# Moving a norm's scale and shift behind a gather, hinting one branch, and reordering the last norm

## The chip, the cores and the metric

The kernel runs on one core of a Trainium2 chip. Times are device microseconds (us) of one launch. The engines are TensorE (PE; its weight loads are PEld), VectorE (DVE), ScalarE (ACT), GpSimd (POOL) and SyncE (SP), which here only issues DMAs. A program with branches runs on every engine's own sequencer; PEq, DVEq and so on name these queues.

## The reference, cut to what matters

One decoder layer on 512 tokens of width 1024, in float32. A token mixer (gated MLP and dilated attention) gives `mix`; then:

```
x = layer_norm(ALPHA * x + g1 * mix, ln1_g, ln1_b)
h = layer_norm(x) * (1 + sc2) + sh2          # second norm, modulated per column
logits = h @ w_router + b_router             # 32 experts, the 4 best of each token
y = sum over the 4 experts of weight * expert(h)      # clamped SwiGLU, 3 matrices of 1024 x 1024
x = layer_norm(ALPHA * x + g2 * y, ln2_g, ln2_b)      # the last norm
```

Only a token's four experts need its row; the kernel reads all 96 weight matrices (4 MB each) once.

## The kernel before, in words

**Routing stage (540 to 635 us).** `layer` works on four blocks of 128 tokens, r = 0 to 3. `mix(r)` is the last projection on TensorE; `norms(r)` makes the first norm, stores ALPHA * x to the DRAM sum `ysum`, and leaves the plain second norm in `h`; `route(r)` transposes `h` on TensorE for the router matmul (whose weights already hold the column scale `sc2`, and whose bias holds `sh2`), then finds the four experts and the slot of every token in its expert's list, on VectorE. For the experts, GpSimd multiplies and shifts `h` in place by rows `sc2` and `sh2` that were broadcast to 128 partitions (L822, L823, names `h<-h,row_sc` and `h<-h,row_sh`), and SP stores it to the DRAM tensor `h2d` (L824). After block 3 the slot table is turned into `gidx` (L946), row numbers for indirect DMAs. The order on each engine in this stage is a scheduler's, by the order of the code and its priorities.

**Experts (635 to 1859 us).** The order of PE, ACT, DVE and SP is as written. For each expert GpSimd gathers up to 128 rows of `h2d` into `xrow` (L1044); `tr_x` transposes them in eight pieces on TensorE (L1057) into two PSUM tiles `ptm` and copies each with one ScalarE copy into `xT` (L1062). `gate`, `up` and `down` multiply with weights that SP's DMAs bring into a ring of 17 buffers of 1 MB (L1024); a buffer is refilled when its last matmul has read it. An expert with up to 64 rows takes `narrow`, one with more takes `wide`; a wide one with over 128 rows takes further blocks (`further`), which gather, transpose and multiply again. The choice is an `If` on a register, labelled `expert{e}`; every engine branches (L1356). `hint(label, ...)` places an instruction on TensorE that names a coming branch; the branches of experts 1 to 31 and of further blocks have one, that of expert 0 has none. While an expert multiplies, `next_rows` already transposes the next one's rows.

**The last norm.** For expert 31 the object `fin` (class `Finish`) loads four blocks of `ysum` rows, x[0] to x[3], by then complete but for expert 31, and normalizes them while expert 31 multiplies. `spread` takes mean and variance on VectorE (`BN_STATS`, L1275) and the root on ScalarE (L1277); `scale` does both steps of the norm on VectorE (L1283, L1284), `scale_act` one pass on ScalarE (L1290) and two on GpSimd (L1291, L1292); `store` writes the rows out. `early` (after the gate) does this for r = 0, 1 with ScalarE and GpSimd, `middle` (in `next_rows`, ahead of `down`) for r = 2, 3 on VectorE. In `y_out`, `add` then joins expert 31's result with the gathered rows that it belongs to, normalizes them and scatters them over `out` (L1333).

Of the kernel before, what the change touches and what calls it, by code (L numbers as in the profile page):

```python
# [9 lines left out]
F32 = mybir.dt.float32  # L10
# [4 lines left out]
AF = mybir.ActivationFunctionType  # L15
ALU = mybir.AluOpType
AX = mybir.AxisListType.X
ET = mybir.EngineType
# [3 lines left out]
P = 128  # L22
H = P // 2
T = 512
D = 1024
KT = D // P
# [43 lines left out]
def layer(tc, I, out, dump=None, n_exp=NE):  # L70
    nc = tc.nc
    V, S, G, PE, SP = nc.vector, nc.scalar, nc.gpsimd, nc.tensor, nc.sync
# [14 lines left out]
    ident = cst[:, :P]  # L87
# [10 lines left out]
    gidx = cp.tile([P, P], I32, name="gidx")  # L98
    wslot = cp.tile([P, P], F32, name="wslot")
# [600 lines left out]
    def row(nm, src):  # L700
        rows[nm] = r4("row_" + nm, 1)
        SP.dma_start(rows[nm], src[0].partition_broadcast(P))

    col2 = f.tile([P, 2, KT], F32, name="col2")
    for i in range(2):
        SP.dma_start(col2[:, i], rowd[1 + i].rearrange("(k p) -> p k", p=P))
    wr = f.tile([P, KT, NE], F32, name="wr")
# [10 lines left out]
    row("sc2", rowd[1:2])  # L718
    row("sh2", rowd[2:3])
# [93 lines left out]
    def route(r):  # L813
# [8 lines left out]
        G.tensor_tensor(h, h, rows["sc2"], op=ALU.mult)  # L822
        G.tensor_tensor(h, h, rows["sh2"], op=ALU.add)  # L823
# [27 lines left out]
        PE.matmul(pcnt, oneb, ohb_, start=r == 0, stop=r == 3)  # L851
# [129 lines left out]
def moe(tc, nc, I, E, main, env):  # L981
    (xrow, land, splA, landB, h2d, ysum, gidx, wslot, gidx2, wslot2, balld, selb, levw, ident, ysv, g2, g2s, yrow, y_init,
     out, epsT, after, last_dve, last_act) = (env[n] for n in (
         "xrow land splA landB h2d ysum gidx wslot gidx2 wslot2 balld selb levw ident ysv g2 g2s yrow y_init out epsT "
# [74 lines left out]
    def tr_x(src, dst):  # L1059
        for a in range(2):  # L1060
            transposes(src[:, 512 * a:512 * a + 512], 4, ptm[a])
            S.copy(dst[:, 4 * a:4 * a + 4], ptm[a])  # L1062
# [139 lines left out]
    def wide(e, lev, levP):  # L1202
        rows_ahead(e, levP)
        gate(e, xT, pg, ga, False, label=f"further{e}_0")
        further(e, 0, lev)
        for q in range(4):
            free(12 * e + q)
        if fin:
            fin.early()
        up(e, xT, pu, ga, aT, False, label=f"further{e}_1")  # L1210
        further(e, 1, lev)
        for q in range(4, 8):
            free(12 * e + q)
        next_rows(e)
        down(e, aT, po, ga, False, free=free, label=f"expert{e + 1}" if e + 1 < E else None)
        y_out(e, 0, po, yrow, False)

    def narrow(e):
        gate(e, xT, pg, ga, True, free)
        if fin:  # L1220
            fin.early()
        up(e, xT, pu, ga, aT, True, free, label=f"expert{e + 1}" if e + 1 < E else None)
        next_rows(e)
        down(e, aT, po, ga, True, free=free)
        y_out(e, 0, po, yrow, True)

    def next_rows(e):
        if e + 1 < E:
            tr_x(xrow, xT)
            if e + 2 < E:  # L1230
                gather(xrow, e + 2, 0)
        if fin:
            fin.middle()
# [7 lines left out]
    class Finish:  # L1241


        def __init__(self):
# [19 lines left out]
            self.mv = [sb.tile([P, 2], F32, name=f"fmv{i}") for i in range(5)]  # L1264
            self.rs, self.nb = (sb.tile([P, 5], F32, name=n) for n in ("frs", "fnb"))
# [27 lines left out]

        def early(self):
            for r in range(2):
                self.spread(r, self.x[r])
            for r in range(2):
                self.scale_act(r, self.x[r])
                self.store(r)

        def middle(self):
            self.fetch(0)
            for r in (2, 3):
                self.spread(r, self.x[r])
                self.scale(r, self.x[r])
                self.store(r)
# [89 lines left out]
```

## Time and profile before

| what | us |
|---|---|
| median of 3 runs | 1881.35 (1880.34 to 1883.35) |
| the profiled execution's own time | 1875.77 |
| its span, first to last instruction | 1874.0 |
| TensorE busy | 1746.6 (93% of the span) |
| VectorE, ScalarE, GpSimd busy | 547.0, 382.3, 201.7 |
| mean granted TensorE clock | 0.974 of full speed |

A busy TensorE says little here, since matmuls are pipelined and weight loads may hold them up; what matters is in which stretches TensorE stands still, and what it then waits for. The DMA rate by slices shows which stretches of the expert loop are fed at the DMA's full rate (some 400 GB/s) and which are not.

### The profile page before, as it was taken

The page shows a single profiled execution, that of the slowest core. Times are in us where ns is not written, and L with a number is a line of the kernel's source. Part 1 is how long each engine was busy: PE and PEld are TensorE (multiplying, and loading weights), DVE is VectorE, ACT ScalarE, POOL GpSimd, SP SyncE. Part 2 cuts the span into 40 slices and gives each one's busy share as a digit, 9 for nine tenths or more (in the row PEclk, how much of TensorE's full clock was granted, in tenths as well). Part 3 has the DMA queues.
Part 4 walks back from the last instruction along what each step waited for, and adds up shares of the span by engine and source line. Part 5 has one row for each costly group of instructions (what it writes and reads, how often), then busy time and mean ns, then how long its engine had stood idle before and what let it go on. Part 6 is the DMA issues. An engine that isn't in the chain of part 4 may idle for free. (4 is left out here: it accounts for less than half of the span.)

```text
span 1874.0 us, 20331 instructions
## 1 busy us (share of the span) xinstructions
PE 1746.6 (93%) x7590; PEld 991.6 (53%) x7590; DVE 547.0 (29%) x901; ACT 382.3 (20%) x745; POOL 201.7 (11%) x152
## 2 busy tenths in 40 slices
PE   6999999999997699999999999998899999899985
PEld 5777778788775444434444444443344444344432
DVE  7546656463279411111111111111011110111115
ACT  3533426255544200100000000011010000000001
POOL 2100000005023300110010001010100000001002
PEclk9999999999999699999999999999999999999998
DMA  8526352423253996999999999999971599949993
GB/s 281 197 88 210 109 191 75 174 68 105 85 187 136 352 366 238 404 404 404 398 390 399 346 380 375 364 399 404 402 284 32 198 401 395 351 170 326 406 384 120
DMA packets 159146, 515.40 MB, mean 275 GB/s; under 512 B 18298, under 2 KB 22858, under 8 KB 158870
## 3 DMA queue, kind: packets, MB, share of 16 engines
q1 hardware_dynamic: 147030, 490.74, 68.3%
q0 software_dynamic: 11840, 21.34, 4.6%
q8 instruction: 128, 2.10, 0.5%
q14 instruction: 148, 1.21, 0.2%
HBM read 504.21 MB, written 23.02 MB: 281 GB/s over the span
## 5 line engine op out<-in xcount | busy, mean ns | idle before, releaser
L1097 ACT ACTIVATE ga<-ga 128x512 f32<-128x512 f32 (+1 forms) x36 | 28.7, 796 | 573.8 <-DVE ga L1096 396.4
L1149 PE MATMUL po<-land,aT 128*128 128x512 f32 x320 | 141.5, 595 | 1.1 <-DVEq L1191 1.1
L166 PE MATMUL mm<-b,splA 128*128 128x512 f32 x352 | 138.8, 394 | 0.0
L167 PE MATMUL mm<-b,splA 128*128 128x512 f32 x352 | 137.9, 392 | 0.0
L168 PE MATMUL mm<-b,splA 128*128 128x512 f32 x352 | 137.8, 392 | 0.0
L1123 PE MATMUL pu<-land,xT 128*64 128x256 f32 x1024 | 129.2, 395 | 8.4 <-DMA land<-in_w_up_dram 8.4
L1091 PE MATMUL pg<-land,xT 128*128 128x512 f32 x288 | 127.7, 599 | 5.1 <-issue 5.1
L1126 PE MATMUL pu<-land,xT 128*128 128x512 f32 x288 | 128.8, 592 | 0.0
L111 DVE TENSOR_TENSOR splA<-land,splA 128x1024 fp32r<-128x1024 f32 x70 | 88.0, 1259 | 130.4 <-ACT splA L110 130.0
L1096 DVE TENSOR_SCALAR ga<-pg 128x512 f32<-128x512 f32 x44 | 30.4, 692 | 317.2 <-PE pg L1091 159.3
L1100 DVE TENSOR_SCALAR pu<-pu 128x256 f32<-128x256 f32 (+1 forms) x64 | 34.1, 533 | 297.6 <-PE pu L1126 160.9
L1088 PE MATMUL pg<-land,xT 128*64 128x512 f32 x504 | 115.3, 608 | 2.6 <-DMA land<-in_w_gate_dram 2.6
L1146 PE MATMUL po<-land,aT 128*64 128x512 f32 x448 | 105.1, 607 | 7.6 <-ACT aT L1107 7.6
L110 ACT CAST splA<-land 128x1024 fp32r<-128x1024 f32 x72 | 75.4, 1051 | 178.1 <-PE mm L168 142.7
L1123 PEld LDWEIGHTS pu<-land,xT 128*64 128x64 f32 x1024 | 74.4, 142 | 53.1 <-DMA land<-in_w_up_dram 13.6
L1107 ACT COPY aT<-ptm 128x256 f32<-128x256 f32 (+1 forms) x64 | 28.9, 451 | 357.8 <-PE ptm L1057 357.8
L1149 PEld LDWEIGHTS po<-land,aT 128*128 128x128 f32 x320 | 59.4, 190 | 70.3 <-issue 67.9
L1091 PEld LDWEIGHTS pg<-land,xT 128*128 128x128 f32 x288 | 55.2, 192 | 72.9 <-issue 70.4
L1044 POOL DMA_INDIRECT xrow<-h2d,gidx x32 | 34.0, 1061 | 541.7 <-PE ptm L1057 530.2
L1126 PEld LDWEIGHTS pu<-land,xT 128*128 128x128 f32 x288 | 53.6, 190 | 66.0 <-issue 64.6
L166 PEld LDWEIGHTS mm<-b,splA 128*128 128x128 f32 x352 | 66.2, 188 | 17.0 <-ACT splA L110 2.6
L1088 PEld LDWEIGHTS pg<-land,xT 128*64 128x64 f32 x504 | 37.0, 140 | 71.2 <-issue 62.4
(379 smaller groups left out, 2514.1 us busy)
## 6 DMA issues: line engine op xcount, KB each, us to landing
land<-in_w_up_dram SPq DMA_DIRECT2D x100, 1024.0 KB, 15.2
land<-in_w_gate_dram SPq DMA_DIRECT2D x99, 1024.0 KB, 18.1
land<-in_w_down_dram SPq DMA_DIRECT2D x96, 1024.0 KB, 18.6
splA<-in_w_down_dram SPq DMA_DIRECT2D x32, 1024.0 KB, 16.4
land<-in_w_in_dram SPq DMA_DIRECT2D x30, 1024.0 KB, 5.2
splA<-in_w_gate_dram SPq DMA_DIRECT2D x29, 1024.0 KB, 20.1
splA<-in_w_up_dram SPq DMA_DIRECT2D x28, 1024.0 KB, 15.8
land<-in_w_ada_dram SPq DMA_DIRECT2D x24, 1024.0 KB, 6.2
```

The costliest lines, as they stand in the source:

```text
L110: hi = S.copy(w[:, 0], src)
L111: return hi, eng.tensor_tensor(w[:, 1], src, w[:, 0].bitcast(F32), op=ALU.subtract)
L166: PE.matmul(o, l[0], r[0], start=start, stop=False)
L167: PE.matmul(o, l[0], r[1], start=False, stop=False)
L168: return PE.matmul(o, l[1], r[0], start=False, stop=stop)
L1088: PE.matmul(r[h], x[:, kt, :H], w[:, :, h], start=False, stop=kt == KT - 1)
L1091: PE.matmul(o[st], x[:, kt], w[:, 512 * st:512 * st + 512], start=False, stop=kt == KT - 1)
L1100: V.tensor_scalar(o, o, LIMIT, -LIMIT, op0=ALU.min, op1=ALU.max)
L1123: PE.matmul(o[st][H * h:H * h + H, :256], x[:, kt, :H], w[:, 256 * h:256 * h + 256], start=False, stop=kt == KT - 1)
L1126: PE.matmul(o[st], x[:, kt], w, start=False, stop=kt == KT - 1)
L1146: end = PE.matmul(o[0][H * n:H * n + H], a[:, 2 * st + b, H * h:H * h + H], wn, start=ft == 0, stop=ft == KT - 1)
L1149: end = PE.matmul(o[n], a[:, ft], wn, start=ft == 0, stop=ft == KT - 1)
```

## The change

Three edits. (1) GpSimd's two passes over `h` and the two row broadcasts go; `h2d` gets the plain second norm, and `tr_x` applies scale and shift while it copies transposed rows: since columns lie on partitions there, the factors are per-partition values, kept in `colh`, a copy of `col2` in a pool that lives on. The first PSUM tile is copied by four ScalarE passes of 128x128, the second by four VectorE passes. (2) A hint for `expert0` stands behind the last count matmul of block 3. (3) In `Finish`, `early` finishes block 0 only; `middle`, now between the next rows and `down`, scales block 1 on VectorE and takes block 2's mean and variance by two ScalarE passes with sums (`spread_act`); `late`, behind `down`, does block 3's on ScalarE and scales 2 and 3 on VectorE.

```diff
+    colh = cp.tile([P, 2, KT], F32, name="colh")
...
+    V.tensor_copy(colh, col2)
...
-    row("sc2", rowd[1:2])
-    row("sh2", rowd[2:3])
...
-        G.tensor_tensor(h, h, rows["sc2"], op=ALU.mult)
-        G.tensor_tensor(h, h, rows["sh2"], op=ALU.add)
         SP.dma_start(h2v[:, r], h)
...
+        cnt = PE.matmul(pcnt, oneb, ohb_, start=r == 0, stop=r == 3)
+        if r == 3:
+            with after(cnt):
+                tc.mark_branch_hint_location("expert0", engines=[ET.PE])
...
     def tr_x(src, dst):
         for a in range(2):
             transposes(src[:, 512 * a:512 * a + 512], 4, ptm[a])
-            S.copy(dst[:, 4 * a:4 * a + 4], ptm[a])
+            for i in range(4):
+                kt = 4 * a + i
+                if a:
+                    V.tensor_scalar(dst[:, kt], ptm[a][:, i], colh[:, 0, kt:kt + 1], colh[:, 1, kt:kt + 1],
+                                    op0=ALU.mult, op1=ALU.add)
+                else:
+                    S.activation(dst[:, kt], ptm[a][:, i], AF.Identity, scale=colh[:, 0, kt:kt + 1],
+                                 bias=colh[:, 1, kt:kt + 1])
...
     def narrow(e):
         gate(e, xT, pg, ga, True, free)
         if fin:
             fin.early()
         up(e, xT, pu, ga, aT, True, free, label=f"expert{e + 1}" if e + 1 < E else None)
         next_rows(e)
+        if fin:
+            fin.middle()
         down(e, aT, po, ga, True, free=free)
+        if fin:
+            fin.late()
         y_out(e, 0, po, yrow, True)
...
+        def spread_act(self, i, x):
+            sm, mv = self.sm[i - 2], self.mv[i]
+            S.activation(self.last[:, 1], x, AF.Identity, accum_out=sm[:, 0:1])
+            S.activation(sm[:, 1:2], sm[:, 0:1], AF.Copy, scale=-1.0 / D)
+            S.activation(mv[:, 0:1], sm[:, 0:1], AF.Copy, scale=1.0 / D)
+            S.activation(self.last[:, 1], x, AF.Square, bias=sm[:, 1:2], accum_out=sm[:, 2:3])
+            S.activation(self.rs[:, i:i + 1], sm[:, 2:3], AF.Sqrt, scale=1.0 / D, bias=epsT)
...
         def early(self):
             for r in range(2):
                 self.spread(r, self.x[r])
-            for r in range(2):
-                self.scale_act(r, self.x[r])
-                self.store(r)
+            self.scale_act(0, self.x[0])
+            self.store(0)
 
         def middle(self):
-            self.fetch(0)
+            self.scale(1, self.x[1])
+            self.store(1)
+            self.spread_act(2, self.x[2])
+
+        def late(self):
+            self.spread_act(3, self.x[3])
             for r in (2, 3):
-                self.spread(r, self.x[r])
                 self.scale(r, self.x[r])
                 self.store(r)
```

`fetch(0)` moves into `next_rows`, where `middle` stood; in `wide` the same calls stand around `further`.

GpSimd's queue in the routing stage, before (`h` with a number is the second norm of one block):

```order
L745 MEMSET ends 128x1 x3
L822 TENSOR_TENSOR h_3810<-h_3810,row_sc_3785 128x1024
L823 TENSOR_TENSOR h_3810<-h_3810,row_sh_3787 128x1024
L822 TENSOR_TENSOR h_3864<-h_3864,row_sc_3785 128x1024
L823 TENSOR_TENSOR h_3864<-h_3864,row_sh_3787 128x1024
L934 TENSOR_TENSOR splA<-xrow,splA 32x1024
L822 TENSOR_TENSOR h_4008<-h_4008,row_sc_3785 128x1024
L823 TENSOR_TENSOR h_4008<-h_4008,row_sh_3787 128x1024
L750 DMA ysum<-xrow,inorder 512x1024
L822 TENSOR_TENSOR h_4143<-h_4143,row_sc_3785 128x1024
L823 TENSOR_TENSOR h_4143<-h_4143,row_sh_3787 128x1024
L1044 DMA xrow<-h2d,gidx 128x1024
```

Now the same stretch of GpSimd's queue has only these:

```order
L745 MEMSET ends 128x1 x3
L935 TENSOR_TENSOR splA<-xrow,splA 32x1024
L750 DMA ysum<-xrow,inorder 512x1024
L1045 DMA xrow<-h2d,gidx 128x1024
L1370 DMA ball<-balld 96x2048
```

Eight passes of 128x1024 are gone; one small pass, on the bias of `down`, stays where it was. The order of DVE, PE and ACT in this stage is the same but for a copy to `colh` and a cast of `trib` that stands two places earlier, both on VectorE.

ScalarE's queue in expert 31, the narrow branch, before (`frs` are the roots, `ga` and `aT` the expert's own data):

```order
L1290 ACTIVATE splA<-splA,fnb,frs 128x1024 x2
L1107 COPY aT<-ptm_4632 128x256
L1277 ACTIVATE frs<-fmv_36169,epsT 128x1
L1277 ACTIVATE frs<-fmv_36170,epsT 128x1
L1107 COPY aT<-ptm_4633 128x256
L1277 ACTIVATE frs<-fmv_36171,epsT 64x1
```

And now:

```order
L1307 ACTIVATE splA<-splA,fnb,frs 128x1024
L1116 COPY aT<-ptm_4623 128x256
L1314 ACTIVATE land_4695,fsm_37657<-splA 128x1024
L1315 ACTIVATE fsm_37657<-fsm_37657 128x1
L1316 ACTIVATE fmv_37654<-fsm_37657 128x1
L1317 ACTIVATE land_4695,fsm_37657<-splA,fsm_37657 128x1024
L1318 ACTIVATE frs<-fsm_37657,epsT 128x1
L1116 COPY aT<-ptm_4624 128x256
L1314 ACTIVATE land_4695,fsm_37658<-splA 128x1024
```

Between the two copies of the expert's transposed activations (`aT`) stood the roots of blocks 2 and 3, whose variances VectorE makes; there stand now two full passes of ScalarE's own, on block 2 alone.

## Rows read from the trace of the kernel before

**Rows 1.** The page's 40 slices of the span: GB/s moved in each.
```profile
GB/s 281 197 88 210 109 191 75 174 68 105 85 187 136 352 366 238 404 404 404 398 390 399 346 380 375 364 399 404 402 284 32 198 401 395 351 170 326 406 384 120
```

**Rows 2.** Stretches: us; PE, PEld, DVE, ACT, POOL busy (instructions), PE clock, DMA share, GB/s.
```profile
597.00:626.00 29.00, 17.24 (x85) 14.07 (x84) 26.86 (x79) 11.28 (x36) 12.95 (x6) 0.62 0.86 291
626.00:642.00 16.00, 6.54 (x21) 4.52 (x23) 6.01 (x17) 2.37 (x8) 3.73 (x4) 0.50 1.04 345
```

**Rows 3.** Instructions on the tile lt in the routing: count, ns min/median/max, first and last start.
```profile
L805 DVE SCALAR_TENSOR_TENSOR lt<-lt,l1sm,row_ln_g x2: 1286/2248/3210, 552.6 to 562.6; 128x1024 f32<-128x1024 f32 x2
...
L805 DVE SCALAR_TENSOR_TENSOR lt<-lt,l1nm,row_ln_g x2: 2856/2898/2939, 580.6 to 599.9; 128x1024 f32<-128x1024 f32 x2
...
L806 DVE SCALAR_TENSOR_TENSOR lt<-lt,l1rs,row_ln_b x4: 1279/2024/3228, 555.4 to 603.3; 128x1024 f32<-128x1024 f32 x4
...
L794 ACT ACTIVATE h<-lt x4: 1044/1058/1061, 549.9 to 569.2; 128x1024 f32<-128x1024 f32 x4
```

**Rows 4.** VectorE in order of time, routing: start us, duration us, line, operation [idle before].
```profile
570.22 0.68 DVE L781 TENSOR_TENSOR h<-mx,land 128x512 f32<-128x512 f32 x1
...
599.94 2.86 DVE L805 SCALAR_TENSOR_TENSOR lt<-lt,l1nm,row_ln_g 128x1024 f32<-128x1024 f32 x1
...
612.49 2.26 DVE L865 TENSOR_TENSOR tA<-cst_s,bk 128x512 fp32r<-128x512 f32 x1
614.67 2.82 DVE L868 TENSOR_TENSOR tC<-cst_s,bk 128x512 fp32r<-128x512 f32 x1
...
617.82 0.18 DVE L830 COPY lg<-pl 128x32 f32<-128x32 f32 x1
```

**Rows 5.** GpSimd in order of time, the same stretch.
```profile
599.36 2.35 POOL L822 TENSOR_TENSOR h<-h,row_sc 128x1024 f32<-128x1024 f32 x1 [6.51 <-PE pt L820]
...
625.37 1.09 POOL L1044 DMA_INDIRECT xrow<-h2d,gidx  x1 [8.42 <-DVE gidx L946]
```

**Rows 6.** TensorE in order of time, the same stretch.
```profile
571.23 0.18 PE L850 MATMUL pl<-ohbf,trib 128*128 128x32 bf16 x1 [2.20 <-DVE ohbf L845]
...
586.20 0.18 PE L850 MATMUL pl<-ohbf,trib 128*128 128x32 bf16 x1 [1.36 <-DVE ohbf L845]
...
615.15 0.63 PE L828 MATMUL pl<-brt,ones 1*128 1x32 f32 x2
```

**Rows 7.** TensorE's queue, branches of three experts (0, 3, 4): ns min/median/max, start us.
```profile
L1356 PEldq COMPARE_BRANCH  x1: 7769/7769/7769, 633.5 to 633.5; - x1
...
L1356 PEldq COMPARE_BRANCH  x1: 351/351/351, 757.2 to 757.2; - x1
...
L1356 PEldq COMPARE_BRANCH  x1: 3067/3067/3067, 780.5 to 780.5; - x1
```

**Rows 8.** TensorE in order of time, at the start of expert 0.
```profile
632.64 1.97 PE L1057 MATMUL ptm<-cst_s,xrow 128*128 128x128 f32 x8 [1.48 <-DMA xrow<-h2d,gidx]
641.42 0.67 PE L1053 MATMUL pg<-ball,selb 96*64 96x512 bf16 x2 [6.82 <-issue]
```

**Rows 9.** All engines in order of time, within expert 1.
```profile
683.52 1.94 PE L1088 MATMUL po<-splA,xT 128*64 128x512 f32 x8 [1.20 <-ACT xT L1062]
...
714.98 0.37 ACT L1107 COPY xT<-ptm 128x256 f32<-128x256 f32 x1 [0.54 <-PE ptm L1057]
```

**Rows 10.** All engines in order of time, expert 31 and the end.
```profile
1842.61 2.37 POOL L1292 TENSOR_TENSOR splA<-splA 128x1024 f32<-128x1024 f32 x1
1842.63 0.42 DVE L1101 SCALAR_TENSOR_TENSOR ga<-pu,ga 128x256 f32<-128x256 f32 x1
...
1844.97 3.39 DVE L1283 SCALAR_TENSOR_TENSOR splA<-splA,fmv 128x1024 f32<-128x1024 f32 x1
...
1853.11 0.29 ACT L1277 ACTIVATE frs<-fmv,epsT 128x1 f32<-128x1 f32 x1 [8.29 <-DVE fmv L1276]
...
1853.71 3.58 PE L1146 MATMUL po<-land,aT 128*64 128x512 f32 x8 [7.65 <-ACT aT L1107]
...
1859.08 0.74 DVE L1327 SCALAR_TENSOR_TENSOR yrow<-po,wslot,g2s 64x512 f32<-64x512 f32 x1 [2.98 <-PE po L1146]
```

More of the change, by code (lines that the diff above doesn't have):

```diff
@@ L850, in route @@
         PE.matmul(pp, trib, ohb_, start=r == 0, stop=True)
-        PE.matmul(pcnt, oneb, ohb_, start=r == 0, stop=r == 3)
+        cnt = PE.matmul(pcnt, oneb, ohb_, start=r == 0, stop=r == 3)
+        if r == 3:
+            with after(cnt):
+                tc.mark_branch_hint_location("expert0", engines=[ET.PE])
         pos = f.tile([P, TOPK], F32, name="pos", bufs=2)
@@ L981, in moe @@
 def moe(tc, nc, I, E, main, env):
-    (xrow, land, splA, landB, h2d, ysum, gidx, wslot, gidx2, wslot2, balld, selb, levw, ident, ysv, g2, g2s, yrow, y_init,
+    (xrow, land, splA, landB, h2d, ysum, gidx, wslot, gidx2, wslot2, balld, selb, levw, ident, ysv, g2, g2s, yrow, y_init, colh,
      out, epsT, after, last_dve, last_act) = (env[n] for n in (
-         "xrow land splA landB h2d ysum gidx wslot gidx2 wslot2 balld selb levw ident ysv g2 g2s yrow y_init out epsT "
+         "xrow land splA landB h2d ysum gidx wslot gidx2 wslot2 balld selb levw ident ysv g2 g2s yrow y_init colh out epsT "
          "after last_dve last_act").split())
@@ L1223, in narrow @@
         next_rows(e)
+        if fin:
+            fin.middle()
         down(e, aT, po, ga, True, free=free)
+        if fin:
+            fin.late()
         y_out(e, 0, po, yrow, True)
@@ L1232, in next_rows @@
         if fin:
-            fin.middle()
+            fin.fetch(0)
     def rows_ahead(e, levP, j=1):
@@ L1264, in __init__ @@
             self.mv = [sb.tile([P, 2], F32, name=f"fmv{i}") for i in range(5)]
+            self.sm = [sb.tile([P, 4], F32, name=f"fsm{i}") for i in range(2)]
             self.rs, self.nb = (sb.tile([P, 5], F32, name=n) for n in ("frs", "fnb"))
```

## The prediction

> **What bounds the kernel now.** I read four views, from coarse to fine. The slices of the page come first [rows 1]: in the expert loop the DMA runs at about 400 GB/s in many slices, but not in the four that hold the routing's end and experts 0 and 1 (136, 352, 366, 238), nor in the last (120). Where weights arrive at full rate, an engine that gets faster gains nothing unless the whole loop starts earlier. So the places to look at are the routing ahead of the loop and the tail behind it, which is where all three edits lie.
>
> Next, the stretches of the routing [rows 2]: from 597 to 626 us VectorE is busy for 26.86 of 29 us and TensorE for 17.24, at a granted clock of 0.62. VectorE bounds this stage. From 626 to 642 neither is busy for even half the time; something else is waited for.
>
> Third, the engines in order of time there. The routing's VectorE passes that read two tensors from SBUF last either 1.28 us or about 3 [rows 3]. One of the long ones started at 599.94 while GpSimd's `h<-h,row_sc` ran from 599.36 to 601.71; it ended at 602.80, 1.09 behind that pass [rows 4, 5]. So it was held until GpSimd was through, and then ran at its usual speed. At 633.5 TensorE's queue meets the branch of expert 0 and spends 7.77 us in it, where a hinted branch to a narrow expert takes 0.35 or 3.07 [rows 7]; the transposes ahead of it end at 634.61, and TensorE stands still for 6.82 us until 641.42, with no releaser but "issue" [rows 8].
>
> Last, the tail. In expert 31 TensorE waits 7.65 us for `aT` [rows 10]. ScalarE could have copied it at about 1845, but in its queue the root of block 3 stands ahead, which waited 8.29 us for VectorE's variance (1853.11). TensorE ends at 1859.0 instead of some 1850, and everything behind it (join, norm, scatter, 14.9 us to the span's end) is late by that.
>
> **The change, part by part.** *Routing.* The eight GpSimd passes go. Blocked VectorE passes get their usual duration: three of L805 (3.21, 2.86, 2.94) and two of L806, the four of which have a minimum of 1.28, a maximum of 3.23 and a median of 2.02, so the two in the middle sum to 4.05 and the second blocked one is 2.77. That is 5.17 + 3.44 = 8.6 us above 1.28 each [rows 3]. Two passes on 128x512, at 612.49 and 614.67, take 2.26 and 2.82 where one of that shape takes 0.68: 3.7 more [rows 4]. The sum is 12.3, but VectorE does not bound everywhere, so I follow the chain.
> - Block 1's two passes give 3.9 by 569 us. The next subtraction from PSUM (L781, 570.22) cannot move before TensorE's projection, which ends at 569.03; that is 1.1 us. TensorE's wait at 571.23 (2.20) shrinks by as much.
> - Block 2's pass at 580.58 gives 1.66. TensorE's wait for VectorE at 586.20 is 1.36 [rows 6], and behind it TensorE is dense; so 1.36 counts.
> - Block 3's passes at 599.94 and 603.32 give 1.58 and 1.48, and nothing else is waited for up to the norm at 608.7: 3.06 in full.
> - The two at 612.49 and 614.67 give 3.7, but the next step (L830, 617.82) needs the router's logits, which end at 615.78 [rows 4, 6]: 2.0 counts, and the logits are then what is late.
>
> Together 7.5 us for the row numbers, the first gather and all behind it. Bounds: 12.3 if TensorE's part moves too, 3 if the cover of TensorE is thicker than I see. The stores of `h` no longer wait for GpSimd in SP's queue, so the weight loads queued behind them go out earlier too. What is added here is one tiny copy to `colh`; it needs `col2`, and the VectorE step behind it then waits for a block of `x` until 547.8 anyway, so it costs nothing; uncovered, it would cost a few tenths.
>
> *The hint.* TensorE can start at 634.7, behind its transposes, if the branch takes 0.35: a gain of 6.7. With 3.07 the queue is free at 636.6 and the gain is 4.8; with nothing gained it is 0. I take 0.35: of the nine branches from one narrow expert to the next, five took 0.34 to 0.36, three 3.0 to 3.1 and one 6.2. What is late next is the first column of `xT`, copied as soon as the first four transposes are through; it hides behind them.
>
> *Does an earlier start come through?* From 626 to 642 the DMA share is 1.04 [rows 2], so the weights could be late instead. But expert 0's are issued before 620, and expert 1 is a wide one: TensorE works on it until 737, and in that slice the DMA falls to 238 GB/s while SP waits for buffers to be freed. That is 47 us x (404 - 238)/404 = 19 us of idle DMA, more than the 14.2 that the start moves by. From there on every load waits for a buffer that is freed earlier by the same amount, so the shift goes to the end.
>
> *`tr_x`.* Per call two copies become four ScalarE and four VectorE passes. In 32 of the 36 calls `down` lies between `xT` and its use. In the four of the further blocks TensorE waits for the first copy (1.20 us, [rows 9]), which is now a quarter of the size. A pass of 128x128 on ScalarE isn't in this trace; by the nearest rows it lies between 0.29 (one column) and 0.59 (four tiles), and two tiles took 0.37 [rows 9, 10]. TensorE uses one column block in 1.94/4 = 0.49. I take 0; bounds are a gain of 4 x 0.3 and a loss of 4 x 1.0.
>
> *Tail.* ScalarE now has one pass fewer before the first `aT` copy and two full ones behind it. With its sum, such a pass takes 1.06 [rows 3] to about 1.4; two and the three small steps make 3.5, from 1840.7 to 1844.3, in time for the second `aT` copy at 1844.6. TensorE then runs through and ends at about 1849.7. VectorE, without block 2 and 3's statistics but with block 1's two passes, is next: its first pass starts at about 1842.7 behind the expert's product [rows 10], is held by GpSimd's second pass until 1844.98 and ends near 1846.2; five more at 1.31 and two reciprocals give 1853.1. The join starts there instead of at 1859.08: 6.0 us. If VectorE's pass comes ahead of GpSimd's instead, the two swap and the sum stays. Bounds: 9.3, if only TensorE's end counted, and 0. The stores of `out` are issued before the join and land under it.
>
> Sum: 7.5 + 6.7 + 6.0 + 0 = 20.2 us. Against the profiled execution, 1875.77 (span 1874.0 and 1.8 around it), that is 1855.6. The median of the runs stands 5.6 above that execution; taken from it, 1881.35 - 20.2 = 1861.2.
>
> **Rivals.** *The hint does nothing.* For it: TensorE passes some 25 instructions of straight code and a wait for the gather between hint and branch, and hinted branches behind a wide expert still take over 5 us in this trace, hidden under queued matmuls. Against it: those of 0.35 stood behind straight code too. Then 13.5 remain: 1867.9. The Trainium skill, page "Runtime: NRT & Kernel Launch", section "Instruction fetch mechanics", says that fetch is purely sequential, two blocks deep, and that a taken branch out of that window must fetch before it goes on. By that rule this rival would hold; the 0.35 us above speak against it.
>
> *The routing's gain is lost at the gather.* It landed 7.3 us after issue (625.37 to 632.64, [rows 5, 8]) with the DMA busy at a share of 0.86 and more. If bytes, not VectorE, set when `xrow` is there, the 7.5 are gone and 12.7 remain: 1868.7. Against it: from 570 to 597 the DMA was mostly idle, and the loads that crowd the gather now go out sooner.
>
> *ScalarE's passes are late in the tail.* If block 2 of `ysum` lands so late that the passes push the second `aT` copy back, TensorE waits as before and the 6.0 are lost: 1867.2. Against it: VectorE read that block at 1842.97 without a wait; passes from then on end at 1846.5, and TensorE at 1851.9, still ahead of VectorE's 1853.1.
>
> *Slower: the hint displaces straight code.* The hinted fetch takes the place of instructions that TensorE needs next, and it stops for each. One uncovered fetch costs up to 7.77 us [rows 7]; the other gains are 20.2, so it decides from the third one on: 20.2 - 23.3, 1884.5. For it only the price; against it, that I found no stall of straight code behind a hint in this trace, which has 55.
>
> **How the numbers follow.** Forecast 0.65, hint without effect 0.14, gather 0.09, tail 0.05, slower 0.04, no effect at all 0.03. The forecast's own range is 1856 to 1866, from 4.8 for the hint up to the routing's other bound. The range of 8 in 10 takes in the rivals at 1867 to 1869 and the spread of runs: 1854 to 1870. A measurement tells 0.2% (3.8 us) from nothing; every case but the last two is beyond it: faster 0.93, same 0.03, slower 0.04.
>
> **What would show it.** In the new profile: no VectorE pass of L805 or L806 above 1.4 us, and the first gather near 617.8; TensorE's gate of expert 0 less than 1 us behind the transposes, near 627; the slice around expert 1 still below 300 GB/s; in expert 31 no wait of TensorE for `aT` above 1 us, VectorE's last `splA` pass directly ahead of the join. Wrong would be a gather that still lands near 632, a branch of 7 us, or an `aT` copy behind 1848 on the old scale.

## The result, and the profile after

The changed kernel takes 1856.51 us (median of four runs, 1856.25 to 1861.74) where the kernel before takes 1880.84 (1879.54 to 1883.35, four runs): a ratio of 0.9876, 95% interval [0.9855, 0.9896]. It is faster, by 24.3 us between the medians; the forecast was 1861.2, from a sum of 20.2 us. The two profiled executions, 1856.64 and 1875.77, differ by 19.1 us. So the sum is nearly right; its terms are less so.

Line numbers of the new kernel differ from the old by -2 to +29. First the routing. The page's GB/s in 40 slices answers [rows 1]; the 16th, within expert 1, is still below 300, as forecast (250).

```profile
GB/s 281 189 103 205 109 183 65 205 46 114 91 160 154 342 383 250 406 406 409 400 394 402 341 388 371 348 403 403 403 284 70 168 396 397 389 161 326 409 401 137
```

The first stretch of [rows 2], and behind it the passes of [rows 3], in the new kernel (columns as there):

```profile
597.00:626.00 29.00, 19.68 (x85) 15.52 (x84) 24.71 (x91) 10.20 (x34) 4.99 (x4) 0.55 0.94 325
```
```profile
L806 DVE SCALAR_TENSOR_TENSOR lt<-lt,l1rs,row_ln_b x4: 1277/1280/1283, 557.1 to 599.7; 128x1024 f32<-128x1024 f32 x4
L805 DVE SCALAR_TENSOR_TENSOR lt<-lt,l1sm,row_ln_g x2: 1285/1285/1285, 554.3 to 564.3; 128x1024 f32<-128x1024 f32 x2
L805 DVE SCALAR_TENSOR_TENSOR lt<-lt,l1nm,row_ln_g x2: 1266/1267/1268, 579.8 to 597.9; 128x1024 f32<-128x1024 f32 x2
```

None of these passes is long any more: the maximum is 1.285 us where it was 3.23. The last block's logits and the first gather, in order of time on VectorE and GpSimd, answer [rows 4, 5]:

```profile
607.57 0.68 DVE L866 TENSOR_TENSOR tA<-cst_s,bk 128x512 fp32r<-128x512 f32 x1
608.17 0.69 DVE L869 TENSOR_TENSOR tC<-cst_s,bk 128x512 fp32r<-128x512 f32 x1
610.70 0.19 DVE L828 COPY lg<-pl 128x32 f32<-128x32 f32 x1 [1.44 <-PE pl L826]
618.13 1.08 POOL L1045 DMA_INDIRECT xrow<-h2d,gidx  x1 [11.08 <-DVE gidx L947]
```

VectorE now waits for the logits, as the forecast said of this place. The gather goes out 7.2 us earlier than at 625.37. The start of expert 0 answers [rows 7, 8] (TensorE's queue, then TensorE):

```profile
L1385 PEldq COMPARE_BRANCH  x1: 6272/6272/6272, 625.9 to 625.9; - x1
```
```profile
625.17 1.97 PE L1058 MATMUL ptm<-cst_s,xrow 128*128 128x128 f32 x8 [1.25 <-DMA xrow<-h2d,gidx]
632.30 0.67 PE L1054 MATMUL pg<-ball,selb 96*64 96x512 bf16 x2 [5.16 <-issue]
```

The hinted branch still takes 6.27 us, and TensorE stands for 5.16 of them. Yet expert 0 starts at 632.30 instead of 641.42: 9.1 us earlier. TensorE's wait for `xT` in a further block, [rows 9] before, is 1.07 instead of 1.20; the four ScalarE passes of 128x128 ahead of it take 1.49 together:

```profile
675.01 1.94 PE L1097 MATMUL po<-splA,xT 128*64 128x512 f32 x8 [1.07 <-ACT xT L1070]
```

In the middle of the loop the gain grows without having been forecast. Expert 31 starts 23.4 us earlier (TensorE at its gate, before and after):

```profile
1826.73 0.39 PE L1053 MATMUL pg<-ball,selb 96*64 96x512 bf16 x2
```
```profile
1803.35 0.39 PE L1054 MATMUL pg<-ball,selb 96*64 96x512 bf16 x2
```

Between 1600 and 1802 TensorE of the kernel before stands three times with no releaser but issue, within one expert's gate and ahead of two others:

```profile
1630.56 11.84 PE L1091 MATMUL pg<-land,xT 128*128 128x512 f32 x23 [3.41 <-issue]
...
1728.00 0.41 PE L1053 MATMUL pg<-ball,selb 96*64 96x512 bf16 x2 [2.59 <-issue]
...
1801.71 0.41 PE L1053 MATMUL pg<-ball,selb 96*64 96x512 bf16 x2 [4.33 <-issue]
```

The same three places in the new kernel have no idle time:

```profile
1616.80 10.46 PE L1100 MATMUL pg<-land,xT 128*128 128x512 f32 x24
...
1710.74 0.39 PE L1054 MATMUL pg<-ball,selb 96*64 96x512 bf16 x2
...
1780.04 0.41 PE L1054 MATMUL pg<-ball,selb 96*64 96x512 bf16 x2
```

The tail gives 4.3 us of it back: from expert 31's first matmul to the join it takes 36.6 us where it took 32.3. All engines in order of time there, answering [rows 10]:

```profile
1804.63 1.55 POOL L1172 DMA_INDIRECT ysum<-yrow,gidx  x1 [21.88 <-DVE gr L1266]
...
1813.12 1.75 SPq L1286 DMA_DIRECT2D splA<-ysum  x4
...
1822.31 1.28 DVE L1292 BATCH_NORM_STATS2 fst<-splA 128x6 f32<-128x512 f32 x2 [9.23 <-DMA splA<-ysum]
...
1826.40 0.66 PE L1058 MATMUL ptm<-cst_s,ga 128*128 128x128 f32 x2 [9.95 <-DVE ga L1110]
...
1827.15 0.37 ACT L1116 COPY aT<-ptm 128x256 f32<-128x256 f32 x1 [0.42 <-PE ptm L1058]
...
1838.79 1.29 DVE L1301 SCALAR_TENSOR_TENSOR splA<-splA,frs 128x1024 f32<-128x1024 f32 x1
1839.99 0.73 DVE L1356 SCALAR_TENSOR_TENSOR yrow<-po,wslot,g2s 64x512 f32<-64x512 f32 x1
```

TensorE's wait for `aT` is gone, and VectorE's last `splA` pass stands directly ahead of the join, as forecast. But the rows of `ysum` are late. The same three steps (expert 30's accumulate, SP's loads, VectorE's first pass on a block) in the kernel before:

```profile
1828.00 1.56 POOL L1163 DMA_INDIRECT ysum<-yrow,gidx  x1 [27.96 <-DVE gr L1250]
...
1831.76 1.75 SPq L1269 DMA_DIRECT2D splA<-ysum  x4
...
1835.16 1.29 DVE L1275 BATCH_NORM_STATS2 fst<-splA 128x6 f32<-128x512 f32 x2 [0.34 <-DMA splA<-ysum]
```

From the accumulate's issue to the loads it takes 8.5 us now and took 3.8; from there to the first block 9.2 now and 3.4. VectorE's statistics, ahead of `act_half` in its queue, wait for it, and TensorE waits 9.95 us for `ga`.

### The profile page after: what moved, and what is told of

Its sections match the earlier page's. It is cut to its first block, busy times and chain, and to the rows that moved or that the text cites. A ratio compares the mean times of both kernels' runs of the same rounds, so it can differ in the third digit from the quotient of the medians.

```text
span 1854.9 us, 20489 instructions
## 1 busy us (share of the span) xinstructions
PE 1742.4 (94%) x7590; PEld 993.2 (54%) x7590; DVE 580.3 (31%) x1041; ACT 402.0 (22%) x828; POOL 175.2 (9%) x142
## 5 line engine op out<-in xcount | busy, mean ns | idle before, releaser
L1132 PE MATMUL pu<-land,xT 128*64 128x256 f32 x1024 | 128.8, 397 | 11.6 <-DMA land<-in_w_up_dram 11.6
```

Of the source, the lines that this page charges most:

```text
L1132: PE.matmul(o[st][H * h:H * h + H, :256], x[:, kt, :H], w[:, 256 * h:256 * h + 256], start=False, stop=kt == KT - 1)
```

## The experiments

Each kernel was timed beside the kernel before; ratios are to it. The table comes from one profiled execution of each: the start of expert 0's gate, and from there to expert 31's gate and to VectorE's first pass on a block of `ysum` (all from the engines in order of time); then from that pass to the join. "Stalls" are the three above. Executions of one kernel differ by some us (1874.10 to 1886.64 over 29 runs of the kernel before), so a column is read over all kernels and not by one pair.

| kernel | gate 0 | to gate 31 | to block 0 | block 0 to join | stalls | ratio [95%] |
|---|---|---|---|---|---|---|
| before | 641.42 | 1185.3 | 1193.7 | 23.9 | yes | 1 |
| hint_only | 642.11 | 1186.1 | 1195.3 | 23.8 | yes | 0.9990 [0.9980, 1.0000] |
| shift_one | 646.30 | 1186.9 | 1196.6 | 24.8 | yes | 1.0005 [0.9993, 1.0016] |
| split_act | 644.28 | 1184.5 | 1193.8 | 23.2 | yes | 1.0000 [0.9987, 1.0013] |
| no_passes | 635.25 | 1185.4 | 1194.7 | 24.6 | yes | 0.9942 [0.9927, 0.9957] |
| order_only | 641.81 | 1181.0 | 1190.0 | 16.5 | yes | 0.9952 [0.9938, 0.9965] |
| half_dve | 641.28 | 1171.7 | 1190.2 | 24.7 | no | 0.9984 [0.9970, 0.9998] |
| idle_passes | 642.05 | 1175.3 | 1196.0 | 23.5 | no | 0.9998 [0.9984, 1.0012] |
| norm_only | 634.43 | 1171.7 | 1191.4 | 24.5 | no | 0.9943 [0.9929, 0.9956] |
| norm_delayed | 630.97 | 1178.5 | 1198.7 | 23.4 | no | 0.9942 [0.9926, 0.9958] |
| after | 632.30 | 1171.1 | 1190.0 | 17.7 | no | 0.9876 [0.9855, 0.9896] |
| fall0 | 629.79 | 1180.9 | 1199.5 | 16.8 | no | 0.9878 [0.9857, 0.9898] |
| tail_late | 631.04 | 1171.4 | 1190.8 | 15.1 | no | 0.9870 [0.9852, 0.9887] |
| hint_late | 632.61 | 1172.4 | 1191.3 | 15.1 | no | 0.9878 [0.9856, 0.9899] |

**One part at a time.** The diffs are the pieces of the change above, each alone on the kernel before; `shift_one` puts one instruction into TensorE's program instead of the hint:

```
 norm_only:  colh, no row sc2/sh2, no G.tensor_tensor on h, tr_x in eight passes
 hint_only:  + mark_branch_hint_location("expert0") behind pcnt of block 3
 order_only: + spread_act, early/middle/late
 shift_one:  + if r == 3 and a == 0:
             +     PE.transpose(pt[:, 3], h[:, 3 * P:4 * P], ident)
```

> The kernel before with the norm's part alone (two GpSimd passes a block out of the routing, scale and shift in the eight transposed copies); TensorE's program is as before. Theory A (the forecast's term): the first gather comes about 7 us earlier, near 618 instead of 625.4, the shift reaches the end, and nothing else changes: about 7.5 us less, 1873. Its branch into expert 0 stays near 7.8 us. Theory B (of the 15 us that the changed kernel gained without forecast between its 1203rd and 1803rd us, in three places where TensorE of the kernel before stands 3.4, 2.6 and 4.3 us for nothing but issue): those three stalls come from when things happen, so 7 us earlier suffices to lose them: 14 to 15 us more, about 1859. Theory C: the stalls come from where TensorE's code lies, which this part does not move: they stay, 1873.

> The kernel before with the hint alone: one instruction more in TensorE's program, ahead of expert 0. Theory A (the forecast's term): the branch of expert 0 falls from 7.77 us to about 0.35, 6.7 us less, 1874. Theory B (the changed kernel's trace, where the hinted branch still takes 6.27 us): the hint gives 1.5 us or nothing, 1879 to 1881. Theory C (the three stalls of 3.4, 2.6 and 4.3 us go because all of TensorE's code behind the hint lies one instruction further): the branch stays at 6 us or more, and yet 12 to 16 us go, 1865 to 1869.

> The kernel before with the last norm's order alone. Theory A (the forecast's term): TensorE's wait of 7.65 us for aT goes, the join is set by VectorE, 6.0 us less, 1875. In the kernel before the ysum rows are asked for at 1831.8 and the first block lands in 3.4 us, so no wait of TensorE for ga over 2 us. Theory B: the new order itself makes TensorE wait about 10 us for ga, as in the changed kernel, where the stretch from expert 31's gate to the join is 4.3 us longer: 1880 to 1885. Under both the three issue stalls of 3.4, 2.6 and 4.3 us between 1600 and 1802 stay, since TensorE's program is as before.

> The kernel before with one transpose of the fourth block done twice (0.1 us of TensorE ahead of expert 0), and nothing else: TensorE's code behind it lies one instruction further, without a hint. Theory C (where the code lies decides whether the three stalls of 3.4, 2.6 and 4.3 us happen): 10 to 15 us less, 1866 to 1871, and the branches at 1721.8 and 1789.6, 6.2 us each, fall to 0.35. Rival (timing, or the hint itself, takes the stalls away): no change beyond 0.1 us, 1880 to 1882, and the stalls are there.

The parts add up: 0.9943, 0.9990 and 0.9952 give 0.9885, the whole has 0.9876. In microseconds of the 1878 that the kernel before had beside them, the norm's part is worth 10.7 (8.3 to 13.3), the hint 1.9 with an interval that ends at nothing, and the order 9.0 (6.6 to 11.6).

`hint_only` falls to its theory B: the branch takes 6.44 us with the hint (first row below), and without one 6.51 in `norm_only` (second) and 6.45 in `order_only` (third). The 7.77 of [rows 7] was that one execution's.

```profile
L1359 PEldq COMPARE_BRANCH  x1: 6441/6441/6441, 635.5 to 635.5; - x1
```
```profile
L1361 PEldq COMPARE_BRANCH  x1: 6509/6509/6509, 627.8 to 627.8; - x1
```
```profile
L1376 PEldq COMPARE_BRANCH  x1: 6452/6452/6452, 635.2 to 635.2; - x1
```

`shift_one` has all three stalls and no gain, so it isn't a matter of where TensorE's code lies by one instruction. The last of them, TensorE in order of time:

```profile
1808.25 0.64 PE L1055 MATMUL pg<-ball,selb 96*64 96x512 bf16 x2 [4.19 <-issue]
```

In `order_only` expert 31 starts late and the rows of `ysum` come early, so no wait of 10 us arises; VectorE from the first block to the join:

```profile
1831.80 1.28 DVE L1283 BATCH_NORM_STATS2 fst<-splA 128x6 f32<-128x512 f32 x2 [0.85 <-DMA splA<-ysum]
...
1848.33 0.74 DVE L1347 SCALAR_TENSOR_TENSOR yrow<-po,wslot,g2s 64x512 f32<-64x512 f32 x1
```

In `norm_only` the stalls are gone, and TensorE's program is that of the kernel before; of the 20.6 us that expert 31 starts earlier, 11.8 are lost again up to the join. Theory B (an earlier start takes the stalls away) was ahead here by the stalls, though the time, 1867.0, lies between its 1859 and the 1873 of the others; it is tested next.

**What takes the stalls away.**

```
 no_passes:    - G.tensor_tensor(h, h, rows["sc2"], op=ALU.mult)
               - G.tensor_tensor(h, h, rows["sh2"], op=ALU.add)
 norm_delayed: norm_only, and ahead of the first tr_x
               + for i in range(7):
               +     held = S.activation(ga, xrow, AF.Copy)
 split_act:    - S.copy(dst[:, 4 * a:4 * a + 4], ptm[a])
               + for i in range(4):
               +     S.copy(dst[:, 4 * a + i], ptm[a][:, i])
 half_dve:     - S.copy(dst[:, 4 * a:4 * a + 4], ptm[a])
               + (V.tensor_copy if a else S.copy)(dst[:, 4 * a:4 * a + 4], ptm[a])
```

> The kernel before without GpSimd's two passes a block, and without anything in their place: it leaves out the second norm's scale and shift in the rows that the experts read. TensorE's, VectorE's and ScalarE's programs are those of the kernel before. The norm's part alone lost 11 us, 7 of them ahead of expert 0 and 13.6 more before expert 31, where three stalls of TensorE (3.4, 2.6, 4.3 us) are gone, and gave 11.8 back in the end. Theory A (the stalls hang on when things happen): 7 us earlier takes them away here too, expert 31's gate starts near 1806 and the time is about 1867. Theory B (they hang on the programs of ScalarE and VectorE, which the norm's part makes longer): the three stalls are here, expert 31's gate starts near 1819, the time is 1870 to 1873. Under both, first gather near 618 to 620, VectorE's passes L805 and L806 at 1.28 us.

`no_passes` starts expert 0 6.2 us earlier than the kernel before, with its copies, and has all three stalls (TensorE in order of time):

```profile
1623.89 11.83 PE L1089 MATMUL pg<-land,xT 128*128 128x512 f32 x23 [3.44 <-issue]
...
1721.32 0.41 PE L1051 MATMUL pg<-ball,selb 96*64 96x512 bf16 x2 [2.58 <-issue]
...
1795.61 0.59 PE L1051 MATMUL pg<-ball,selb 96*64 96x512 bf16 x2 [4.90 <-issue]
```

So theory A falls: the earlier start isn't it. Its time is nevertheless that of `norm_only` (0.9942 and 0.9943), though expert 31 starts 14.5 us later in the one than in the other. What TensorE gained between experts 0 and 31 was worth nothing that these two kernels can tell.

> The norm's part alone, with seven passes of ScalarE over the gathered rows (1.06 us each) ahead of the first transposes: expert 0 starts 7.4 us later, near 642, as in the kernel before; TensorE's program is as before. Theory A (when things happen decides on the stalls): with the start of before the three stalls are back, expert 31's gate starts near 1826, the time is near 1878. Theory B (the programs of ScalarE and VectorE decide): no stalls, expert 31's gate near 1813.5; since the end then gives back less, 1870 to 1874.

This one failed as a delay. The seven passes lie under the branch, which takes 6.13 us at the same time, so TensorE's first weight matmul waits only 0.39 us for `xT` (ScalarE, then TensorE):

```profile
624.04 7.58 ACT L1351 ACTIVATE ga<-xrow 128x1024 f32<-128x1024 f32 x7 [3.85 <-DMA xrow<-h2d,gidx]
...
632.03 2.83 PE L1093 MATMUL pg<-land,xT 128*64 128x512 f32 x6 [0.39 <-ACT xT L1066]
```

It says nothing on the stalls. It does show that 7 us of ScalarE's time are free there as long as the branch costs 6.

> The kernel before, its copies of transposed rows cut from two of 128x512 into eight of 128x128, all on ScalarE; TensorE's and VectorE's programs are as before. Without GpSimd's passes the three stalls stayed; with the norm's part they went, so they hang on the copies. Theory A (ScalarE's longer program or later copies decide): the stalls of 3.4, 2.6 and 4.3 us are gone here, expert 31's gate 12 to 14 us earlier than before (1813 instead of 1826.7); TensorE waits up to 2 us longer for xT in the further blocks. Theory B (the half on VectorE decides): the stalls stay, 1878 to 1890.

> The kernel before, with the second of the two copies of transposed rows on VectorE instead of ScalarE, whole as it is. Theory A (ScalarE's program decides, by being longer): the three stalls stay, about 1878. Theory B (that half of the copies is VectorE's): the stalls are gone, expert 31's gate near 1813, the time 1868 to 1872 since the end gives part of it back.

Eight passes on ScalarE leave the stalls as they are; one of the two copies on VectorE takes all three away. The last place in `split_act`, and the first two in `half_dve` (TensorE in order of time):

```profile
1803.76 0.41 PE L1053 MATMUL pg<-ball,selb 96*64 96x512 bf16 x2 [4.30 <-issue]
```
```profile
1627.13 5.31 PE L1091 MATMUL pg<-land,xT 128*128 128x512 f32 x12
...
1720.39 0.39 PE L1053 MATMUL pg<-ball,selb 96*64 96x512 bf16 x2
```

All six kernels of the table with both copies on ScalarE have the stalls, and all eight with half on VectorE have not, in one profiled execution of each. Where two of the three arise can be seen: ahead of the second and of the third stands a hinted branch of TensorE's queue that takes 5.6 to 6.3 and 6.1 to 6.9 us in the six, and 0.4 to 3.1 and 0.3 to 0.8 us in the eight. The second stall's branch in `split_act` and in `half_dve`:

```profile
L1357 PEldq COMPARE_BRANCH  x1: 6289/6289/6289, 1723.7 to 1723.7; - x1
```
```profile
L1356 PEldq COMPARE_BRANCH  x1: 3072/3072/3072, 1716.9 to 1716.9; - x1
```

The first stall lies in the straight code of a gate. How VectorE's half shortens the branches and takes that stall away, no row shows; it stays open. Its worth is 0.9984, 3.0 us with an interval from 0.4 to 5.6 (expected were 7 to 11), although expert 31 starts 13.6 us earlier behind expert 0.

**Why an earlier expert 31 is worth so little.** From expert 0's gate to the first block of `ysum` it takes 1194.0 us in the mean of the six kernels with stalls (1190.0 to 1196.6) and 1193.5 in that of the eight without (1190.0 to 1199.5), while expert 31's gate comes 10.8 us earlier in the mean (1184.9 and 1174.1). The 150 us ahead of the accumulate's landing, in the kernel before and in the changed one (stretches: us; PE, PEld, DVE, ACT, POOL busy, PE clock, DMA share, GB/s):

```profile
1680.00:1830.00 150.00, 141.74 (x648) 61.73 (x646) 18.93 (x38) 12.37 (x24) 13.72 (x10) 0.99 0.98 372
```
```profile
1664.00:1814.00 150.00, 148.02 (x701) 65.54 (x702) 27.07 (x61) 15.97 (x37) 13.82 (x11) 1.00 0.98 375
```

The DMA share is 0.98 in both. TensorE is busy for 142 us of one and for 148 of the other, and the bytes differ by under 1%: here the weights set the pace, and two of the three stalls lie within. A TensorE that is ahead issues its accumulate while expert 31's weights are still queued: in the eight kernels without stalls it takes 7.8 to 8.6 us from there to SP's loads and 8.9 to 10.9 more to the first block, in the six with stalls 3.8 to 5.5 and 2.9 to 3.9. In the changed kernel the first block lands at 1822.3 whether TensorE waits for `ga` or, as in `tail_late` (1821.8), does not.

About half of the DMA is free by then. Around the issue of the loads (1813.12) its share in the changed kernel is 0.48:

```profile
1811.00:1814.00 3.00, 3.00 (x30) 1.97 (x28) 0.69 (x1) 0.78 (x2) 0.14 (x1) 1.00 0.48 187
```

What is late is one part of each load. A load lands in sixteen parts, and the trace has the time of each: of the first block fifteen are there between 1815.90 and 1817.45 and the sixteenth at 1822.29; of the last 1 MB of weights, issued some 16 us ahead of it, fifteen by 1813.65 and the sixteenth at 1817.28. So, as far as these times tell, one share of the queue still had weights, and the last norm's two rows behind them, to move. The sixteenth part of the first block comes 2.5 to 5.7 us behind the fifteenth in the eight kernels without stalls, and at most 0.6 behind it in the six with them. Why one share falls behind the others stays open.

**The routing.**

```
 idle_passes: norm_only, and behind the store of h
              + scr = f.tile([P, D], F32, name="scr", bufs=1)
              + G.tensor_tensor(scr, h, rows["ln1_g"], op=ALU.mult)
              + G.tensor_tensor(scr, scr, rows["ln1_b"], op=ALU.add)
```

> The norm's part alone, with GpSimd still making two passes a block of the old size beside the routing, from the block into a tile that nobody reads; the block's store no longer waits for them. From the routing's first subtraction (L781) to the first gather lie 81.0 to 82.6 us in the kernels with the old norm and 72.1 to 76.1 in those with the new one. Theory A (the forecast's: the passes cost by the time that VectorE's passes beside them take): VectorE's L805 and L806 are back at 2.2 to 2.9 us beside them, the stretch is back at 78 to 82 us, the time near 1872. Theory B (they cost because the store and so the gather waited for them): the stretch stays at 72 to 76 us, 1867.

The time is back at 0.9998, and the whole gain of the norm's part with it; both theories had less (1872 and 1867). From L781 to the gather it takes 79.6 us, as theory A had it, which is most of the way back, and three of VectorE's eight passes of L805 and L806 are long again, at 3.18, 2.16 and 2.02 us (VectorE on the tile `lt`):

```profile
L806 DVE SCALAR_TENSOR_TENSOR lt<-lt,l1rs,row_ln_b x4: 1273/1282/3181, 559.6 to 607.2; 128x1024 f32<-128x1024 f32 x4
L805 DVE SCALAR_TENSOR_TENSOR lt<-lt,l1sm,row_ln_g x2: 1283/1720/2157, 556.8 to 566.9; 128x1024 f32<-128x1024 f32 x2
L805 DVE SCALAR_TENSOR_TENSOR lt<-lt,l1nm,row_ln_g x2: 1267/1641/2015, 583.8 to 605.4; 128x1024 f32<-128x1024 f32 x2
```

Nothing waits for these passes' results, and between 545 and 628 us no other engine's wait ends with a pass of GpSimd. So theory B falls: they cost by standing beside VectorE.

**The branch, and the tail.**

```
 fall0:     no hint, and for e == 0
            + with tc.If(lev < 1, preferred_fallthrough_block=True) as more:
            +     narrow(e)
            + with more.Else():
            +     wide(e, lev, levP)
 tail_late: the changed kernel with, in narrow(e),
              up(...); next_rows(e); down(...)
            + fin.early(); fin.middle(); fin.late()
 hint_late: tail_late, the hint behind the last matmul of y_init(3)
```

> The changed kernel without the hint and with the two bodies of expert 0 exchanged: its narrow body, which it takes, falls through; the jump now stands behind it, over the wide body. In the changed kernel the hinted branch takes 6.27 us, and the first matmul of expert 0 starts 4.5 us behind the last copy of xT (627.8). Theory A (those 6.3 us are the fetch of code that lies far off, which the hint didn't bring in): the gate of expert 0 starts within 1 us of the copies, 3.5 to 4.5 us earlier, and the jump is hidden by the 6.4 us of down that TensorE still has queued; 1852 to 1853 if the end lets it through, 1855 to 1857 if the end gives it back, as it did with most of what the norm's part gained. Theory B (the jump costs the same at its new place): a stall of 3 to 6 us ahead of expert 1's gate, 1856 to 1858. Theory C (TensorE waits there for something else, the register loads or the weights): the gate stays near 632.

Theory A holds for the gate and B for the rest. Without the taken branch TensorE starts 2.8 us behind the start of the transposes instead of 7.1, and the jump over the wide body then costs 2.67 us ahead of expert 1 (TensorE in order of time):

```profile
629.79 0.67 PE L1051 MATMUL pg<-ball,selb 96*64 96x512 bf16 x2 [0.87 <-DVE xT L1064]
...
658.45 0.77 PE L1047 MATMUL pg<-ball,selb 96*128 96x512 bf16 x2 [2.67 <-issue]
```

Its time, 0.9878, is not to be told from the changed kernel's. Its profiled execution, 1862.74, is the slowest of its five (1850.76 to 1862.74), and the 1180.9 and 1199.5 of the table are that one's.

> The changed kernel (1856.5) with all of the last norm's work on the four blocks written behind the last expert's down, so that no instruction that waits for the blocks' rows stands ahead of the passes that TensorE waits for. In the changed kernel the rows land at 1822.3 and TensorE waits 9.95 us for ga behind VectorE's statistics; the join comes at 1840.0. Theory A (that wait and what it pushes sets the end): TensorE is done with down near 1827, VectorE has 2 x 1.5 us of statistics and 3 x 2.6 us of scaling behind 1822.3, the join near 1834: 6 us less, 1850.5. Theory B (the blocks' late rows set the end by VectorE and ScalarE alone, TensorE is hidden behind them): ScalarE's chains for blocks 2 and 3, 3.0 us each, end no sooner, the join at 1838 to 1840, 0 to 2 us less. Slower (1858) if the last down's own first half now comes behind ScalarE's long passes.

TensorE's wait is gone, and it is through with `down` at 1824.7 instead of 1838.5. The join comes only 3.1 us earlier, between the two theories; by time, 1855.2, theory B is nearer (TensorE, then VectorE):

```profile
1815.46 0.44 PE L1058 MATMUL ptm<-cst_s,ga 128*128 128x128 f32 x2
...
1821.81 1.29 DVE L1290 BATCH_NORM_STATS2 fst<-splA 128x6 f32<-128x512 f32 x2 [3.53 <-DMA splA<-ysum]
...
1826.50 3.26 DVE L1299 SCALAR_TENSOR_TENSOR splA<-splA,frs 128x1024 f32<-128x1024 f32 x1
...
1836.87 0.74 DVE L1354 SCALAR_TENSOR_TENSOR yrow<-po,wslot,g2s 64x512 f32<-64x512 f32 x1
```

The 14 us of TensorE were nearly all hidden: VectorE works from the first block's landing to the join with hardly a pause, and two of its passes are 2 us longer beside GpSimd's. This kernel is the fastest of the study by its median, 1855.2, but its interval covers the changed kernel's.

> The changed kernel with the last norm's work behind the last down (1855.2), and with the hint moved from the last count's matmul, 13.4 us ahead of expert 0's branch, to behind the last matmul of the rows' bias, some 3 us ahead of it. Theory A (an early hint is lost by the time of the branch): a late one counts, the branch falls by up to 3 us, from 6.2 to 3 or 3.5; the gate of expert 0 starts 3 us earlier. Theory B (the hint doesn't bring this code in at all): 6.2 us as with the early hint (6.27, 6.44) and without one (6.45, 6.51).

The late hint stands 4.9 us ahead of the branch in TensorE's queue (621.3 and 626.2), not 3, and does as little as the early one:

```profile
L1383 PEldq COMPARE_BRANCH  x1: 6291/6291/6291, 626.2 to 626.2; - x1
```

## Why the prediction was right, and where not

*The sum.* In the two profiled executions the join moves by 19.1 us: 9.1 up to expert 0's gate, 3.7 from there to the first block of `ysum`, 6.2 from there on. The forecast had 14.2, 0 and 6.0. By the parts timed alone, the norm's part gave 10.7 for a forecast of 7.5, the hint 1.9 for 6.7 and the order 9.0 for 6.0: 21.6 against 20.2. So the sum came out by luck: the hint's shortfall of 4.8 was made up by two terms that were sized too small. Of the 4.7 us by which the median fell below the forecast, 2.5 are the base's doing: the kernel before takes 1874 to 1887 us from run to run, with a median of 1878.87 over 29 runs, and the forecast was taken from 1881.35.

*Routing, 7.5.* Right in mechanism, somewhat small. The gather moves by 7.2 us although the stage begins 1.7 us later in the changed kernel's execution (L781 at 546.05, before at 544.36), so the stretch between them is 8.9 us shorter; between kernels it is 81.0 to 82.6 against 72.1 to 76.1. `idle_passes` shows that standing beside GpSimd makes most of what the stretch gains, and in time all that the norm's part gains: 0.9998 with the passes, 0.9943 without, some 10 us. The step at the logits came out as written: they are what is late there now.

*Hint, 6.7.* Wrong; the rival "the hint does nothing" was right. The step that failed is the choice of 0.35 us by the branches from one narrow expert to the next. Hinted, this branch takes 6.2 to 6.4 us in four kernels, and unhinted 6.1 to 6.5 in seven of nine, 6.99 and 7.77 in the others. The branch of 6.2 us that the forecast counted among its nine and passed over is the second stall's, hinted too. By the rule of the Trainium skill, page "Runtime: NRT & Kernel Launch", section "Instruction fetch mechanics", a taken branch to code that isn't at hand must fetch it first; the trace agrees at this branch (6.27 us hinted, and 0.87 of waiting for `xT` where `fall0` lets the code follow straight on), and not at the narrow ones of 0.35. The 1.65 us by which the start of expert 0 still gained on its transposes is mostly the distance to the 7.77 of that execution. That a hint brings this code in at all, no run shows.

*Does an earlier start come through?* Yes for what comes ahead of expert 0, as forecast: the time from its gate to the first block stays at 1190 to 1200 us, wherever in 629.8 to 646.3 it starts. Hardly for what is gained within the loop; that case was not in the forecast.

*`tr_x`, 0.* In the four further blocks TensorE's waits are shorter by 0.1 us each, within the bounds. What was overlooked is that half of the copies on VectorE takes three stalls out of TensorE: 13.6 us at expert 31, worth 3.0 us of time in `half_dve` and none to be seen in `idle_passes`.

*Tail, 6.0.* Right by size: block 0 to join is 23.2 to 24.8 us in the nine kernels with the old order and 16.5 to 17.7 in the three with the new. Alone it is worth 9.0 us, with an interval from 6.6 to 11.6. `aT` and the last `splA` pass stand as forecast; ScalarE's two passes and three small steps took 3.0 us (1827.42 to 1830.41), not 3.5. That TensorE "then runs through" was wrong: it waits 9.95 us for `ga`, which `tail_late` shows to cost little, since VectorE sets the end, as the forecast had it, from the landing of the first block on.

*Rivals.* The gather didn't eat the routing's gain: it lands 7.0 us after issue, 7.3 before. Between the new hint and expert 0's gate TensorE has no other idle time put down to issue than the branch's, and `hint_only` is not slower. But the forecast's ground against this rival was misread: the 3.41 us at 1630.56 are a stall of straight code, 11 us behind a hint in TensorE's queue (1619.3).

## What to carry to other kernels

A stall of the busiest engine is worth what the next landing behind it lets through: measure from the start of the loop to that landing before counting it. A mean DMA share under 1 does not say that a load is free to land: look at when the last of its parts does. Before a GpSimd pass is kept because nothing waits for it, look at what VectorE's passes of known length do beside it. A hint's effect is read from a branch of the same place and distance, not from the best hinted branch of the program.

## What the runs showed of the hardware that was not expected

Which engine makes a small copy can decide on stalls of another that have no releaser but issue: three of TensorE's, 3.4, 2.6 and 4.3 us, stood in six kernels and were absent in eight, and `half_dve` took them away by VectorE's half of the copies alone. The hinted branch ahead of the third went from 6.1 us or more to 0.8 or less with them. A hint 4.9 us or 13.5 us ahead of a branch left it at 6.29 and 6.27 us. The same load of a 512 KB block was there 3.4 us after issue behind a nearly empty queue, and 9.2 us after it where one of its sixteen parts had weights ahead of it; the other fifteen were there after 4.3. Four passes of 128x128 from PSUM with a scale and a shift of their own took 1.50 us on ScalarE and 1.37 on VectorE.
